# A hybrid attention block on one core: first-stage weights split earlier, dummies between two turns, latent keys and values one step sooner, latent weights by two loads

## The chip, the cores and the metric

The kernel runs on one core of one Trainium2 chip. The metric is device time in microseconds (us) of that core; lower is better. The time shown is the median of several runs on the chip, beside one further execution that was profiled and from which all rows of the trace come.

## The reference

A decoder block of depth 1 on 512 tokens of width 1024, with 16 learned tokens put in front (528 in all). In short:

```
u    = rmsnorm(h)                         # 528 x 1024
proj = u @ w_in                           # cq, ckv, k_pe, z_mla, fq, fk, fv, f, z_fox, gate_a, gate_b
q    = rmsnorm(cq) @ w_uq                 # MLA: 16 heads of 64 + 32 (rotated)
k, v = rmsnorm(ckv) @ w_ukv               # MLA: 16 heads of 64 and 64, the rotated key shared
o_mla = causal_attention(q, k, v)
o_fox = causal_attention(fq, fk, fv, with a cumulative forget gate)   # 16 heads of 64
y_mla = (o_mla * silu(z_mla)) @ w_br_mla ;  y_fox = (o_fox * silu(z_fox)) @ w_br_fox
h    += rmsnorm((sigmoid(gate_a) * y_mla + sigmoid(gate_b) * y_fox) @ w_out)
```

All in float32. `w_uq` is 256 x 1536 (16 heads of 64 + 32 columns) and `w_ukv` 128 x 2048 (16 heads of 64 key and 64 value columns). The 16 added tokens are dropped from the output.

## The kernel before

**Precision.** TensorE multiplies in a reduced float32. Each product is therefore made of three matmuls: operands are split into a high half (a cast copy) and a low half (the difference), and high x high, high x low and low x high are added in PSUM. For weights a unit loads a raw tile (`wload`, L105), casts it on ScalarE to `wh` and subtracts on GpSimd to `wl` (`wsplit`, L125). Raw, `wh` and `wl` tiles have three buffers each. `weights` (L137) makes a `get` that loads and splits once, with `get.load` for the load alone.

**Units and steps.** `unit` (L175) cuts one projection into steps of three matmuls. Its first step calls `getw()`, the split, and starts the loads of the next three units (`nxt`, set by `ahead`, L842); its last step calls `done`, which evicts the PSUM bank. The banks for these results, `acc` (L170), are three. So `z` (8 steps of 512 columns), `mq` (the MLA query, 2 steps), `mk` (MLA key, 2 short steps in two banks), `v` and so on are lists of steps, and a stage strings such lists together in a `fill`.

**Phases.** The first phase normalises the input, turns it (`turn`, L355: eight transposes by TensorE of one block of 128 tokens), and makes the small projections (`small`, L391, into `psm`; `back`, `latent`). Ten dummy matmuls into `spun` (L450) run before. Then come 16 stages, alternately forgetting attention (FoX, `br` 1) and MLA (`br` 0) for each of 8 pairs of heads. Stage 0 is FoX of pair 0, stage 1 MLA of pair 0, stage 2 FoX of pair 1, and so on. At last the branch products (`py`) and the output product (`x`, `y`, `z` tiles of that phase) follow.

**A stage** (L888 on) issues scores `s0`, the values `va` of the stage before (`late`), scores `s1`, then the steps of its `fill`, with the normalisations `n0` and `n1` (L778) put among them. The scores (`st` on TensorE) go through VectorE (`sf`, the negated maximum) and ScalarE (exponential). `norm` writes the probabilities in two half-precision halves (`pn`: high on ScalarE L801, low on VectorE L802, the first 16 keys on GpSimd L788 to L793), and starts transposing DMAs from `pn` to `pt` on the SyncE queue, two per block of 128 queries, eight per stage. `values` (L812, `ov` on TensorE) multiplies `pt` by the values `vp`, which another transposing DMA makes from `vh`. `n0` covers the first three query blocks, `n1` the fourth.

**The fill.** A FoX stage prepares its own and the next stage's gates and the MLA operands:

```
fill = (vts[br, pr] if pr else begun) + za + q + zb[:4] + k + zb[4:6] + v + zb[6:]
```

`za` is `z` of the FoX branch, `zb` of the MLA branch, `q` is `mq`, `k` is `mk` and `v` the MLA values. An MLA stage has `fq`, `fk` and `v` of the next pair. In stage 0, `fill[:5]` is issued ahead of `n0`: four steps of a gate unit (`pg`) and the first of `za`; `n0` and `n1` follow directly, and then `fill[5:]`.

**Values and z.** `v_unit` (L664) finds a power-of-two scale `vsc` on VectorE from the largest entry (L679 to L687), then writes `vh` on ScalarE (L692, L698) and VectorE (L701). `z_unit` (L710) evicts `z` as `sil` by ScalarE (L714) and VectorE (L715). `hl_done` (L234) evicts queries and keys (`hlq`, `hlk`) by ScalarE and VectorE, with a raised priority.

**What sets the order.** On TensorE the order is that of the program, written out by hand. On ScalarE, VectorE, GpSimd and partly SyncE a planner puts instructions in order by their estimated readiness and priority (`high_priority` raises it, `issue_after` makes one follow another; `pin` and `keep_in_program_order` fix the order). Each engine then runs its list strictly in that order.

**The latent weights.** `q_mla` (L579) loads, for one pair of heads, four pieces: for each of the two halves of `w_uq` 64 columns of two heads, and from `w_ukv` the key and the value columns of the two heads (512 columns in all). One cast and one subtraction split them.

Of the kernel before, what the change touches and what calls it, by code (L numbers as in the profile page):

```python
# [12 lines left out]
F32R = mybir.dt.float32r  # L13
# [18 lines left out]
NOPE = 64  # L32
ROPE = 32
HD = 64
# [15 lines left out]
def f32(ap):  # L50
    return ap.bitcast(F32)
# [3 lines left out]
def block_kernel(ctx: ExitStack, tc: tile.TileContext, x, meta_tokens, pre_norm_g, w_in, fox_forget_b,  # L55
                 mla_q_norm_g, mla_kv_norm_g, w_uq, w_ukv, w_br_mla, w_br_fox, w_out, post_norm_g,
                 rope_tok, rope_pe, out):
    nc = tc.nc
# [5 lines left out]
    wuq = w_uq[0].rearrange("(k p) f -> p k f", p=128)  # L64
    wukv = w_ukv[0]
# [17 lines left out]
    wp = ctx.enter_context(tc.tile_pool(name="wp", bufs=3))  # L83
    uid = [0]
    written, sums_out = [False], []
    behind, through, first_t, exps, halved, lowered = [], [], [], [], {}, {}
# [9 lines left out]
    def mm(*a, **k):  # L96
        nc.tensor.matmul(*a, **k)  # L97

    def tps(*a):
        nc.tensor.transpose(*a)  # L100

    def split_lo(eng, lo, src, hi):
        return eng.tensor_tensor(out=lo, in0=src, in1=f32(hi), op=ALU.subtract)  # L103

    def wload(srcs):  # L105

        uid[0] += 1
        u = uid[0]
        raw = wp.tile([128, 1024], F32, tag="wraw", name=f"wraw{u}")
        n = 0  # L110
        parts = []
        for src in srcs:
            dims = src.shape[1:]
            w = int(np.prod(dims))
            names = "abcd"[: len(dims)]
            pat = f"p ({' '.join(names)}) -> p {' '.join(names)}"
            rv = raw[:, n : n + w].rearrange(pat, **{c: d for c, d in zip(names, dims)})
            dma(rv, src)
            parts.append((n, w))
            n += w  # L120
        return u, raw, parts, n
# [15 lines left out]
    def weights(srcs, wrap):  # L137

        st = {}

        def load():
            if "l" not in st:
                st["l"] = wload(srcs())

        def get():
            load()
            return wrap(wsplit(st["l"]))
        get.load = load
        return get
# [20 lines left out]
    def acc(name):  # L170
        return accp.tile([128, 512], F32, tag="acc", name=name)
# [3 lines left out]
    def unit(name, getw, act, nk, sls, done):  # L175

        st = {}
        out = []
        for i, sl in enumerate(sls):
            n = sl.stop - sl.start  # L180
            for k in range(nk):
                def fn(i=i, sl=sl, k=k, n=n):
                    if "w" not in st:
                        st["w"] = getw()
                        for load in getattr(out[0][1], "nxt", ()):
                            load()
                    if k == 0:
                        st["ps"] = acc(f"{name}{i}")
                    ps = st["ps"][:, :n]
                    (wh, wl), (ah, al) = st["w"], act(k)  # L190
                    for q, (w, a) in enumerate(((wh, ah), (wh, al), (wl, ah))):
                        mm(ps, w(k), a[:, sl], start=(k == 0 and q == 0), stop=(k == nk - 1 and q == 2))
                    if k == nk - 1:
                        done(i, ps)
                out.append((3 * n / 2.4, fn))
        if hasattr(getw, "load"):
            out[0][1].load = getw.load
        return out
# [25 lines left out]
    CT = fx.tile([128, L], F32R, tag="CT", name="CT")  # L224
    ONE = fx.tile([128, 128], F32R, tag="ONE", name="ONE")
# [40 lines left out]
    with ExitStack() as ph:  # L266
# [64 lines left out]
        def squares(t, pin):  # L331

            rows = 128 if t < 4 else META
            ht = hts[t]
            hn = hns[t] = pa.tile([128, D], F32, tag="hn", name=f"hn{t}", bufs=3)
            st1 = sts[t] = pa.tile([128, 16], F32, tag="st1", name=f"st1_{t}")
            if t == 0:

                for i, sl in enumerate(halves):
                    pin(nc.scalar.activation(hn[:, sl], ht[:, sl], AF.Square, accum_out=st1[:, 2 + i : 3 + i]))  # L340
                pin(nc.vector.tensor_scalar(out=st1[:, 0:1], in0=st1[:, 2:3], scalar1=1.0 / D, scalar2=EPS, op0=ALU.mult,
                                            op1=ALU.add))
                pin(nc.scalar.activation(st1[:, 1:2], st1[:, 3:4], AF.Sqrt, bias=st1[:, 0:1], scale=1.0 / D))
                pin(nc.vector.reciprocal(st1[:, 1:2], st1[:, 1:2]))
            else:
                pin(nc.scalar.activation(hn[:rows], ht[:rows], AF.Square, accum_out=st1[:rows, 0:1]))
                rstd(st1[:rows, 1:2], st1[:rows, 0:1], D, 0, rows, pin)
# [7 lines left out]
        def turn(t):  # L355
            rows = 128 if t < 4 else META
            for half in range(2):

                pt = acc(f"pt{t}_{half}").rearrange("p (a b) -> p a b", a=4) if t in (1, 4) else \
                    ppt.tile([128, 4, 128], F32, tag="pt", name=f"pt{t}_{half}")  # L360
                pts0[t, half] = pt
                for kk in range(4):
                    k = 4 * half + kk
                    tps(pt[:, kk, :rows], hns[t][:rows, 128 * k : 128 * k + 128], ident[:rows, :rows])
# [84 lines left out]
        spun = acc("spun")  # L449
# [5 lines left out]
        scaled(0, pin)  # L455
        pin(nc.vector.tensor_copy(gcol, gps[:, 0, 0:KD]))
        turn(0)
        squares(1, pin)
        scaled(1, pin)
        pin(small_hi(0, nc.scalar.copy))  # L460
# [87 lines left out]
    with ExitStack() as att:  # L548
# [25 lines left out]
        wuqh = wuq.rearrange("p k (h e) -> p k h e", e=NOPE + ROPE)  # L574
# [2 lines left out]
            dma(f32(QP), qpe_dram[2 * pr : 2 * pr + 2].rearrange("h i x f s -> (h i x f) s"))  # L577

        def q_mla(pr):  # L579
            kv = wukv.rearrange("p (h a e) -> p a h e", a=2, e=HD)  # L580

            def wrap(w):
                mw[pr] = w
                return (lambda k: w[k][0]), (lambda k: w[k][1])
            get = weights(lambda: [wuqh[:, k, 2 * pr : 2 * pr + 2, 0:NOPE] for k in range(2)]
                          + [kv[:, i, 2 * pr : 2 * pr + 2, :] for i in range(2)], wrap)

            halves = hl_done(("q", 0, pr), S, S)

            def q_done(i, ps):  # L590
                halves(i, ps)
                if pr:
                    load_qp(pr)
            return unit(f"mq{pr}", get, cq_act, 2, REAL, q_done)
# [62 lines left out]
        mw = {}  # L657
# [175 lines left out]
        vts = {}  # L833
# [18 lines left out]
        begun = g[4:]  # L852
        fills = []
        for si, (br, pr) in enumerate(stages):
            last = si + 1 == len(stages)
            if not last:
                q, k, v = feed(*stages[si + 1])
            if br == 1:

                za, zb = z_unit(1, pr), z_unit(0, pr)  # L860
                fill = (vts[br, pr] if pr else begun) + za + q + zb[:4] + k + zb[4:6] + v + zb[6:]
            elif not last:

                fill = vts[br, pr] + q + k[:KD] + v + k[KD:]
            else:
                g = gate_unit()
                fill = vts[br, pr] + g + gate_unit() + gate_unit()
            if si == 5:
                pe, rest1, _ = pe_unit(1)
                fill[17:17] = pe  # L870
            fills.append(fill)
# [16 lines left out]
        for si, (br, pr) in enumerate(stages):  # L888
            s0, s1, n0, n1, va = attention(br, pr)

            fill = fills[si]
            for fn in [s0] + late:
                fn()
            if si == 0:
                run(fill[:3])
            s1()

            if si == 0:

                run(fill[3:5])  # L900
                run(vts[1, 0] + pe_rest)
                n0()
                n1()
                first_t.extend(through)
                run(fill[5:])
            else:
                if si == 1:

                    written[0] = True
                    for x in range(2):  # L910
                        store0(x, 2, 8)
                    written[0] = False
                run(fill[:5])
                if si == 1:

                    behind[:] = exps[:1]
                if si == 2:
                    behind.clear()
                n0()
                run(fill[5:11])  # L920
                if br:

                    behind[:] = [halved[("k", 1, pr), 1]]
                run(fill[11:12])
                if br:
                    behind.clear()
                n1()
                if 6 <= si < 8:

                    written[0] = True  # L930
                    rest1(si - 6)
                    written[0] = False
                run(fill[12:])
            written[0] = False
            if si == 1:

                behind[:] = [halved[("k", 1, 1), 0]]
            late = [va]
# [232 lines left out]
```

## Time and profile before

| | us |
|---|---|
| median of 3 runs | 606.51 |
| lowest and highest | 606.22 and 607.24 |
| the profiled execution's own time | 607.8 |
| its span, from first to last instruction | 606.0 |
| VectorE busy | 370.6 |
| ScalarE busy | 343.3 |
| GpSimd busy | 179.0 |

In the profile PE is TensorE's matmuls, PEld its weight loads, DVE is VectorE, ACT ScalarE, POOL GpSimd, SPq the SyncE queue that issues DMAs. A row of a timeline has the start, the duration, the engine, the line, the operation, what is written and read, the shape, the count, and in brackets the idle time of the engine before it and what ended it. A row of the waits has the waiting engine, tile and line, what it waited for, then the total, the count and the longest. A row of a group ends with busy time and mean ns of one, then idle time before them with its causes. TensorE's matmuls overlap, so a matmul's duration is longer than the step from one start to the next.

### The profile page before, as it was taken

What the parts mean: (1) busy time and instruction counts of PE and PEld (TensorE: products, weight loads), DVE (VectorE), ACT (ScalarE), POOL (GpSimd) and SP (SyncE); (2) the same over time, 40 slices, a digit from 0 to 9 for tenths busy, and PEclk for the clock granted to TensorE, in tenths of its full rate; (3) what the DMA queues carried; (4) which work ended last, traced back from release to release, by engine and by line L of the source; (5) the groups of instructions that cost most, each with busy time, mean ns of one, the idle gap of its engine ahead of it and who ended that gap; (6) DMA issues with size and microseconds to landing.
All of it is one profiled execution on the core that took longest, in us unless ns stands there. A gap on an engine that the chain in (4) does not pass through costs nothing.

```text
span 606.0 us, 11016 instructions
## 1 busy us (share of the span) xinstructions
PE 593.3 (98%) x3773; PEld 502.2 (83%) x3773; DVE 370.6 (61%) x1002; ACT 343.3 (57%) x780; POOL 179.0 (30%) x231
## 2 busy tenths in 40 slices
PE   7999999999999999999999999999999999999996
PEld 5889789789889889888798898887888888888884
DVE  4956657765775674675666557683823624367857
ACT  7847755764774685675666658671221533243653
POOL 4316626443438444353433534530000000000000
PEclk9999999999999999999999999999999999999999
DMA  8433689989798788999787786997634333332603
GB/s 292 101 89 82 132 191 166 225 175 211 118 179 162 163 191 160 193 178 191 144 151 178 148 175 158 192 167 249 210 105 104 94 82 104 104 93 92 233 0 138
DMA packets 225335, 92.71 MB, mean 153 GB/s; under 512 B 141868, under 2 KB 217012, under 8 KB 225280
## 3 DMA queue, kind: packets, MB, share of 16 engines
q1 hardware_dynamic: 225280, 92.03, 66.9%
q8 instruction: 29, 0.48, 0.3%
q14 instruction: 26, 0.21, 0.1%
HBM read 57.57 MB, written 4.00 MB: 102 GB/s over the span
## 4 chain that ended last, share of the span: by engine, by line
PE 88%; ACT 3%; DVE 3%; DMA 2%; issue 2%; POOL 0%; SPq 0%; DVEq 0%; ACTq 0%
PE z L97 15%; PE py L97 14%; PE pg L97 14%; PE v L97 9%; PE fk L97 8%; PE fq L97 7%; PE st L97 6%; PE ov L97 4%; PE x L97 4%; PE psm L97 2%; DVE sf L766 2%; PE mq L97 2%; PE mk L97 1%; DMA wsr<-in_w_in_dram 1%; PE ppe L97 1%
## 5 line engine op out<-in xcount | busy, mean ns | idle before, releaser
L130 ACT CAST wh<-wraw 128x1024 fp32r<-128x1024 f32 (+1 forms) x88 | 87.9, 1001 | 155.2 <-PE v L97 46.3
L103 POOL TENSOR_TENSOR wl<-wraw,wh 128x1024 fp32r<-128x1024 f32 (+1 forms) x55 | 121.3, 2207 | 106.6 <-ACT wh L130 106.4
L774 ACT ACTIVATE sf<-sf,nb 128x144 f32<-128x144 f32 (+3 forms) x128 | 72.0, 564 | 13.3 <-DVE nb L766 13.3
L802 DVE SCALAR_TENSOR_TENSOR pn<-sf,ri,pn 128x128 f16<-128x128 f32 (+3 forms) x128 | 68.7, 576 | 13.3 <-ACT pn L801 13.2
L801 ACT ACTIVATE pn<-sf,ri 128x128 f16<-128x128 f32 (+3 forms) x128 | 61.5, 551 | 20.4 <-ACT sf L774 17.3
L103 DVE TENSOR_TENSOR wl<-wraw,wh 128x1024 fp32r<-128x1024 f32 x33 | 40.3, 1222 | 41.3 <-ACT wh L130 41.2
L97 PE MATMUL z<-uTh,wl 128*128 128x512 f32 x128 | 50.2, 392 | 1.6 <-POOL wl L103 1.6
L97 PE MATMUL z<-uTh,wh 128*128 128x512 f32 x128 | 50.9, 398 | 0.0
L766 DVE CUSTOM_DVE_ANT_0 sf<-st,maskt 128x272 f32<-128x272 f32 (+2 forms) x128 | 48.5, 434 | 3.9 <-PE st L97 3.9
L97 PE MATMUL pg<-uTh,wh 128*128 128x512 f32 x128 | 50.3, 393 | 0.0
L97 PE MATMUL z<-uTl,wh 128*128 128x512 f32 x128 | 50.0, 391 | 0.0
L97 PE MATMUL pg<-uTl,wh 128*128 128x512 f32 x128 | 49.8, 389 | 0.0
L97 PE MATMUL pg<-uTh,wl 128*128 128x512 f32 x128 | 49.8, 389 | 0.0
L97 PE MATMUL py<-gh,wh 128*128 128x512 f32 x128 | 49.8, 389 | 0.0
L97 PE MATMUL py<-gl,wh 128*128 128x512 f32 x128 | 49.8, 389 | 0.0
L97 PE MATMUL py<-gh,wl 128*128 128x512 f32 x128 | 49.8, 389 | 0.0
L97 PE MATMUL st<-hlk,hlq 64*128 64x272 f32 (+3 forms) x480 | 49.1, 308 | 0.3
L97 PEld LDWEIGHTS st<-hlk,hlq 64*128 64x128 f32 x480 | 36.0, 185 | 7.0 <-ACT wh L130 2.5
L97 PE MATMUL v<-uTh,wh 128*128 128x256 f32 (+1 forms) x128 | 36.5, 285 | 0.0
L97 PE MATMUL v<-uTh,wl 128*128 128x256 f32 (+1 forms) x128 | 36.5, 285 | 0.0
L97 PE MATMUL fk<-uTl,wh 128*128 128x256 f32 (+1 forms) x128 | 36.4, 285 | 0.0
L97 PE MATMUL fk<-uTh,wh 128*128 128x256 f32 (+1 forms) x128 | 36.4, 285 | 0.0
(232 smaller groups left out, 1403.4 us busy)
## 6 DMA issues: line engine op xcount, KB each, us to landing
wraw<-in_w_in_dram SPq DMA_DIRECT2D x56, 512.0 KB
wraw<-in_w_br_fox_dram SPq DMA_DIRECT2D x8, 512.0 KB
tb<-in_w_out_dram SPq DMA_DIRECT2D x8, 512.0 KB
wraw<-in_w_br_mla_dram SPq DMA_DIRECT2D x8, 512.0 KB
wraw<-in_w_out_dram SPq DMA_DIRECT2D x6, 512.0 KB
pt<-pn SPq DMA_TRANSPOSE x128
xr<-in_x_dram SPq DMA_DIRECT2D x4, 512.0 KB
out_dram<-yo SPq DMA_DIRECT2D x8, 256.0 KB
```

What stands on the lines that cost most here:

```text
L97: nc.tensor.matmul(*a, **k)
L103: return eng.tensor_tensor(out=lo, in0=src, in1=f32(hi), op=ALU.subtract)
L130: nc.scalar.copy(wh[:, :n], raw[:, :n])
L766: nc.vector.tensor_tensor_reduce(out=sf_of(h, b)[:, c0 : c0 + w], in0=ps[h][:, o : o + w], in1=maskt[:, m0 : m0 + w], scale=-scale, scalar ...
L774: exps[g] = nc.scalar.activation(sf, sf, AF.Exp, bias=sums["nb"][:, h, b : b + 1], scale=-1.0, accum_out=sums["su"][:, h, b : b + 1]).ins
L801: nc.scalar.activation(hi, sf, AF.Copy, scale=rib)
L802: nc.vector.scalar_tensor_tensor(out=lo, in0=sf, scalar=rib, in1=hi, op0=ALU.mult, op1=ALU.subtract)
```

## The change

Four edits. (1) Each unit's first step gets a function `prep` that makes the split ahead of the step; in stage 0 the first two units of `fill[5:]` (`mq0` and the first `zb`, called `z00`) are prepared between `n0` and `n1`. (2) Four more dummies into `spun` follow `turn(0)`. (3) In a FoX stage `k` and `v` come one `zb` step sooner. (4) `q_mla` loads two pieces, 192 columns from each half of `w_uq` (with the 32 rotated ones per head, which aren't used here) in one DMA and 256 adjacent columns of `w_ukv` in another, 640 columns in all. Two casts and two subtractions pick the 512 wanted ones out.

```diff
@@ unit
+        def prep():
+            if "w" not in st:
+                st["w"] = getw()
+            return True
...
-                    if "w" not in st:
-                        st["w"] = getw()
+                    if "b" not in st:
+                        st["b"] = prep()
                         for load in getattr(out[0][1], "nxt", ()):
                             load()
...
+        out[0][1].prep = prep
@@ first phase
         turn(0)
+        for _ in range(4):
+            mm(spun, ONE, CT[:, 0:512], start=True, stop=True)
         squares(1, pin)
@@ q_mla
-            kv = wukv.rearrange("p (h a e) -> p a h e", a=2, e=HD)
-
-            def wrap(w):
-                mw[pr] = w
+            ld = []
+
+            def load():
+                if not ld:
+                    ld.append(wload([wuq[:, :, 192 * pr : 192 * pr + 192], wukv[:, 256 * pr : 256 * pr + 256]]))
+
+            def get():
+                load()
+                u, raw, _, _ = ld[0]
+                wh, wl = (wp.tile([128, 1024], F32R, tag=t, name=f"{t}{u}") for t in ("wh", "wl"))
+                cuts = [(raw[:, 0:384].rearrange("p (b e) -> p b e", e=96)[:, :, 0:NOPE], lambda t: t[:, 0:256].rearrange("p (b e) -> p b e", e=NOPE)),
+                        (raw[:, 384:640].rearrange("p (h a e) -> p a h e", h=2, a=2), lambda t: t[:, 256:512].rearrange("p (a h e) -> p a h e", a=2, h=2))]
+                for src, to in cuts:
+                    with tc.issue_after(behind[0]) if behind else nullcontext():
+                        nc.scalar.copy(to(wh), src)
+                for src, to in cuts:
+                    split_lo(nc.gpsimd, to(wl), src, to(wh))
+                w = mw[pr] = [(wh[:, o : o + 128], wl[:, o : o + 128]) for o in range(0, 512, 128)]
                 return (lambda k: w[k][0]), (lambda k: w[k][1])
-            get = weights(lambda: [wuqh[:, k, 2 * pr : 2 * pr + 2, 0:NOPE] for k in range(2)]
-                          + [kv[:, i, 2 * pr : 2 * pr + 2, :] for i in range(2)], wrap)
+            get.load = load
@@ fill of a FoX stage
-                fill = (vts[br, pr] if pr else begun) + za + q + zb[:4] + k + zb[4:6] + v + zb[6:]
+                fill = (vts[br, pr] if pr else begun) + za + q + zb[:3] + k + zb[3:5] + v + zb[5:]
@@ stage 0
                 n0()
+                for ahead_ in [fn.prep for _, fn in fill[5:] if hasattr(fn, "prep")][:2]:
+                    ahead_()
                 n1()
```

## The prediction

> **What bounds the kernel now.** I read the page's busy times first, then the waits of TensorE, then the timelines around each of those waits, engine by engine.
>
> ```profile
> PE 593.3 (98%) x3773; PEld 502.2 (83%) x3773; DVE 370.6 (61%) x1002; ACT 343.3 (57%) x780; POOL 179.0 (30%) x231
> ```
>
> ```profile
> PE z L97 <- POOL wl L103: 1.6, 1, 1.6
> PE ov L97 <- DMA pt<-pn: 0.9, 2, 0.5
> PE ov L97 <- issue: 0.7, 2, 0.4
> ```
>
> TensorE is busy for 98% of the span, so the change can only win what TensorE idles, and it adds no matmul but four dummies. The largest waits are one for a low half of weights (1.6 us, in stage 0) and two sets in front of `ov`, the product of probabilities and values. Matmuls that start late without an idle row cost a little more; I find those by comparing equal stretches, below.
>
> **Part 1: weights ahead of the last normalisation.** The 1.6 us wait, with what ScalarE and GpSimd did before it:
>
> ```profile
> 64.78 1.30 POOL L103 TENSOR_TENSOR wl<-wraw,wh 128x512 fp32r<-128x512 f32 x1
> ...
> 71.33 1.34 ACT L801 ACTIVATE pn<-sf,ri 128x512 f16<-128x512 f32 x2 [0.47 <-DVE ri L783]
> 72.57 1.03 ACT L130 CAST wh<-wraw 128x1024 fp32r<-128x1024 f32 x1
> ...
> 73.68 2.37 POOL L103 TENSOR_TENSOR wl<-wraw,wh 128x1024 fp32r<-128x1024 f32 x1 [1.44 <-ACT wh L130]
> ...
> 74.14 0.39 PE L97 MATMUL z<-uTl,wh 128*128 128x512 f32 x1
> 76.11 0.50 PE L97 MATMUL z<-uTh,wl 128*128 128x512 f32 x1 [1.57 <-POOL wl L103]
> ```
>
> ```profile
> 112.39 5.65 PE z L97 x24
> ```
>
> The row from the chain has 24 matmuls of 512 columns in 5.65 us: one starts 0.235 us after another, so the one at 76.11 was due at 74.14 + 0.23 = 74.37: 1.74 us are lost. Of the two units prepared early, `mq0` is halved early in the old order already (512 columns, on GpSimd until 66.08); `z00` is the one that counts. Its cast now precedes the two `pn` of `n1` (1.34 us). ScalarE is free 0.47 us before 71.33, at 70.86, so the cast ends about 71.9 and the subtraction, 2.37 us later, about 74.3, when TensorE wants it: −1.74 us in stage 0. The four small GpSimd pieces of `n1` come either before or after it; if before, some 0.3 us of the wait stay. What is pushed back is `n1`: its `pn` come about 1.1 us later, and their two transposing DMAs are the last of eight in a row on the SyncE queue, which holds 11.10 us from 69.22 and reaches the seventh at 69.22 + 6 x 1.39 = 77.6. `pn` is done by 75, so nothing is late there.
>
> The Trainium skill ("SBUF — State Buffer", section "Who interferes with whom") says that a VectorE instruction with two SBUF inputs and a GpSimd instruction that reads SBUF exclude one another. By it the moved subtraction would hold `pn` on VectorE (1.42 us) until 74.3, and `hlq` behind it until 77.1, so that `mk` would wait 0.7 us for its bank and part 1 would be worth −1.0 instead of −1.74; the sum would stay, since stage 1 keeps less than that of either (part 2), but a sum in which stage 1 keeps all would be 0.7 us poorer. The trace agrees with the rule in this row against this mean, while a GpSimd subtraction ran from 90.48:
>
> ```profile
> 91.31 1.91 DVE L802 SCALAR_TENSOR_TENSOR pn<-sf,ri,pn 128x256 f16<-128x256 f32 x1
> ...
> L802 DVE SCALAR_TENSOR_TENSOR pn<-sf,ri,pn 128x256 f16<-128x256 f32 x32 | 17.3, 561 | 0.0
> ```
>
> **Part 2: how much of it survives stage 1, and the two loads.** The next wait of TensorE is at the values of stage 1, and it hangs on the SyncE queue:
>
> ```profile
> 69.22 11.10 SPq L91 DMA_TRANSPOSE pt<-pn  x8
> 80.37 1.27 SPq L91 DMA_DIRECT2D wraw<-in_w_in_dram  x2
> 81.69 4.50 SPq L91 DMA_DIRECT2D qpe_dram<-gT  x4
> ...
> 87.12 3.07 SPq L91 DMA_TRANSPOSE vp<-vh  x1
> ...
> 91.69 2.87 SPq L91 DMA_TRANSPOSE pt<-pn  x2
> 94.65 1.05 SPq L91 DMA_DIRECT2D wraw<-in_w_uq_dram  x2
> 95.80 1.21 SPq L91 DMA_TRANSPOSE pt<-pn  x1
> 97.06 1.08 SPq L91 DMA_DIRECT2D wraw<-in_w_ukv_dram  x2
> 98.25 4.57 SPq L91 DMA_TRANSPOSE pt<-pn  x3
> 102.90 0.53 SPq L91 DMA_DIRECT2D wraw<-in_w_in_dram  x1
> 103.60 3.45 SPq L91 DMA_TRANSPOSE pt<-pn  x2
> ```
>
> ```profile
> 108.39 0.38 PE L97 MATMUL ov<-pt,vp 80*64 80x512 f16 x1 [0.48 <-DMA pt<-pn]
> 109.19 2.03 PE L97 MATMUL ov<-pt,vp 80*64 80x512 f16 x25 [0.42 <-DMA pt<-pn]
> ```
>
> The reader is to see that the queue has hardly a gap from 69 to 107: each row starts where the one before ended (the two rows left out fill 86.3 to 87.0 and 90.3 to 91.5). The last two transposes go out from 103.60 on, and TensorE waits for the landing of the one at 108.39 and of the other at 109.19. So up to 109.19 the queue, not TensorE, sets the time, and what stage 0 wins would only lengthen these two waits. But the four loads of `mq1` stand in this queue, ahead of those transposes: from 94.65 to 95.80 and from 97.06 to 98.25, 2.34 us. With two loads instead of four I take half away, 1.17 us. From above: those loads bring 128 x 8 runs of 64 numbers, the new ones 128 x 3 of 192 or 256, and a transpose just behind the loads is slower (three of them in 4.57 us, against 3 x 1.21), so up to 0.94 us more may go, 2.1 us. From below: if the queue's pace is set by the transfers and not by the issues, nothing. I take 1.17, as the nearest rows have it. The second wait then ends at 108.0, and TensorE, there 1.74 us earlier, does wait: parts 1 and 2 together give −1.17 us, and the other 0.57 us of part 1 are given back.
>
> In later pairs a shorter queue wins only where TensorE waits for it; the waits above name four in front of `ov`, two of them these, so I take nothing there. The cast of `mq` becomes two casts of 256 columns and two subtractions. What a second instruction adds, from rows of 512 and 1024: on ScalarE 2 x 0.63 − 1.03 = 0.23 us, on GpSimd 2 x 1.30 − 2.37 = 0.23 us. The old casts stand where ScalarE had been idle:
>
> ```profile
> L130 ACT CAST wh<-wraw 128x512 fp32r<-128x512 f32 x10 | 6.3, 627 | 38.5 <-PE v L97 34.6 <-issue 3.6 <-PE z L97 0.2
> ```
>
> That idle time, 38.5 us before ten casts, hides them; without it the two would cost 0.46 us a pair, 3.7 us in all.
>
> **Part 3: latent keys and values one z step sooner.** A z step is three matmuls, 0.7 us. The order of TensorE's work changes but not its amount. At the start of an MLA stage the rows are these:
>
> ```profile
> 126.18 0.16 DVE L687 RECIPROCAL vsc<-vsc 128x1 f32<-128x1 f32 x1
> 126.29 1.05 ACT L130 CAST wh<-wraw 128x1024 fp32r<-128x1024 f32 x1 [0.22 <-PE z L97]
> 127.24 0.59 ACT L714 ACTIVATE sil<-z 128x512 f32<-128x512 f32 x1
> 127.73 0.28 ACT L692 ACTIVATE vh<-v,vsc 128x32 f16<-128x32 f32 x1
> ...
> 130.63 0.72 PE L97 MATMUL st<-hlk,hlq 64*128 64x272 f32 x6
> 132.48 0.50 PE L97 MATMUL fq<-uTh,wh 128*128 128x512 f32 x1
> ...
> 173.22 0.65 PE L97 MATMUL st<-hlk,hlq 64*128 64x272 f32 x6
> ...
> 174.63 0.50 PE L97 MATMUL fq<-uTh,wh 128*128 128x512 f32 x1
> ```
>
> The second cast waits for the end of `z` and holds `sil` and the eviction of the values (`vh`) behind it; VectorE's `sf` comes after both, and the scores wait for a PSUM bank: 130.63 to 132.48 is 1.85 us. In the stage at 173.22, where the second cast has only 512 columns, the same stretch is 1.41. So 0.44 us go in each stage of the slow kind; four stretches of that length are in the timeline, from 130.63, 218.11, 346.26 and 388.77: 1.76 us. The scale of the values (`vsc`) is ready at 126.34 now, just after `z` ends at 126.3. With `v` 0.7 us sooner it is ready about 125.65, and the order of ScalarE, which is planned by when work comes ready, should put `vh` into the idle time there and leave only the cast and `sil` behind `z`. VectorE then does `vh` a microsecond sooner and reaches `sf` about 1.5 us sooner, more than the 0.44 us: −1.76 us. If the order on ScalarE stays, `vh` still waits behind the cast and nothing is won. What is queued behind: the second cast slips by up to 0.7 us, for `fk`, whose matmuls come 6 us later.
>
> The price is in PSUM. `mk` takes over the banks of `mq` and of the z before. In stage 4:
>
> ```profile
> 163.47 0.68 DVE L103 TENSOR_TENSOR hlq<-mq,hlq 128x512 fp32r<-128x512 f32 x1
> ...
> 164.94 0.28 PE L97 MATMUL mk<-cTh,wh 128*128 128x256 f32 x1
> ```
>
> `mq` is evicted at 164.15; `mk`'s second half, moved to 164.94 − 0.69 = 164.25 (three matmuls of 0.23), comes 0.10 us after that. It fits, barely. I take the five FoX stages after it as like it, cost it at nothing, and at most 0.1 us x 6 for the release itself.
>
> **Part 4: four dummies.** `turn(1)` waits for `hn`, and TensorE is idle for 0.59 us before it:
>
> ```profile
> 2.07 4.63 PE L97 MATMUL spun<-CT,ONE 128*128 128x512 f32 x10 [2.07 <-DVE ONE L230]
> ...
> 8.77 1.09 PE L100 MATMUL pt<-ident,hn 128*128 128x128 f32 x8 [0.59 <-DVE hn L352]
> ...
> 12.81 2.17 ACT L376 ACTIVATE uTh<-pt,gcol 128x128 fp32r<-128x128 f32 x8
> ```
>
> At 0.23 us each they end at 9.1, at the 0.46 of the first ten at 10.0: `turn(1)` ends up to 1.3 us later, at most 11.2, and ScalarE reads it at 12.81. Nothing is lost, and as the cast of the last weights, not TensorE, sets when ScalarE comes to it, nothing is won: 0, from −0.2 to +0.3.
>
> **Sum.** −1.17 − 1.76 = −2.9 us. The profiled execution took 607.8 us, of which the span is 606.0; it lies 1.3 us above the median, 606.51, and the terms are taken off that median: 603.6 us, a span of 603.1.
>
> **Rivals.**
> *The transfers, not the issues, pace the queue.* Then two loads win nothing there, and all of part 1 is given back at 109: 606.5 − 1.76 = 604.7 us. For it: transposes behind loads are slower than others. Against: between the loads they go at 1.21 each, as fast as any. The Trainium skill ("DMA: Bandwidth & Descriptors", section "Anatomy of one DMA — SWDGE (gpsimd) path") has the fixed cost of a DMA mostly in its completion and little in its issue; by that this rival's time would hold, but the rows above show half a microsecond of the queue for each.
> *ScalarE's order stays.* `vh` remains behind the cast; only −1.17: 605.3 us. For it: in the old order it stands there although its scale was ready at 126.34, and the new 125.65 may not count for the planner.
> *Both:* 606.5, no change, and the change doesn't do what it says.
> *Slower: the bank of `mq` isn't free.* The margin is 0.10 us. If the new order puts one cast of 1.05 us ahead of `hlq` on ScalarE, `mk` waits 0.95 us in each of six stages: +5.7 − 2.9, 609.3 us. It decides from a delay of more than 0.10 us, and loses from 0.6 us on. For it: ScalarE is in order and its order is made anew; against: the eviction has a raised priority.
>
> **How the numbers follow.** Forecast 603.6: 0.42; transfers 604.7: 0.15; ScalarE's order 605.3: 0.18; both fail 606.5: 0.10; slower 609.3 or on the way there: 0.15. 0.2% is 1.2 us, about what can be told from no change; the boundary, 605.3, halves the third case. Faster 0.42 + 0.15 + 0.09 = 0.66, same 0.09 + 0.10 = 0.19, slower 0.15. The range: below, 2.1 for the queue plus 1.76 plus what shorter waits before `ov` elsewhere may give (0.7 us), 602.0; above, no gain and the bank's 0.6 us, 607.1. It leaves out most of the slower case.
>
> **What would show it.** Right: no row of `z` waiting for `wl` near 74; two loads of `in_w_uq` and `in_w_ukv` for each pair and the second wait of `ov` ending near 108.0; `vh` ahead of `sil` on ScalarE, and 1.41 us from `st` to `fq` in all MLA stages. Wrong: a new wait of `mk` for `hlq` or `sil`; the `ov` of stage 1 still at 109; longer waits of `ov` in later FoX stages, where the old ones (0.7 us in two) show how tight the landing is.

## The result, and the profile after

| | us |
|---|---|
| after, median of 13 runs | 604.04 (602.86 to 607.24) |
| before, median of 13 runs, the three of 606.51 among them | 607.62 (606.22 to 609.08) |
| ratio after to before, 95% interval | 0.9949 (0.9936 to 0.9963) |
| the profiled execution after, its span | 603.71, 601.8 |

The change makes the kernel faster by 0.5%: 0.0051 x 607.62 = 3.1 us, from 2.2 to 3.9 by the interval. Forecast were 2.9 us and 603.6. In the profiles of after and of the experiments some lines have other numbers: `pn` is L822 and L823, `sil` L735 and L736, `vh` L713, L719 and L722, the VectorE `sf` L787.

Busy times and the waits of TensorE, after. A row of the waits has the total, the count and the longest:

```profile
PE 592.5 (98%) x3777; PEld 501.7 (83%) x3777; DVE 374.1 (62%) x1002; ACT 343.9 (57%) x788; POOL 180.6 (30%) x239
```

```profile
PE ov L97 <- DMA pt<-pn: 0.3, 1, 0.3
PE z L97 <- POOL wl L103: 0.3, 1, 0.3
```

The 1.6 us wait for `wl` has become 0.3, and the 1.6 us in front of `ov` have become 0.3. Part 1, in the timeline of stage 0 after:

```profile
70.67 1.04 ACT L130 CAST wh<-wraw 128x1024 fp32r<-128x1024 f32 x1
...
71.29 0.24 POOL L809 TENSOR_TENSOR mt<-sf,ri 128x32 f32<-128x32 f32 x1 [3.62 <-DVE ri L804]
...
72.11 2.40 POOL L103 TENSOR_TENSOR wl<-wraw,wh 128x1024 fp32r<-128x1024 f32 x1
...
72.36 3.37 DVE L823 SCALAR_TENSOR_TENSOR pn<-sf,ri,pn 128x512 f16<-128x512 f32 x2 [1.22 <-ACT pn L822]
...
73.90 0.39 PE L97 MATMUL z<-uTl,wh 128*128 128x512 f32 x1
74.57 0.50 PE L97 MATMUL z<-uTh,wl 128*128 128x512 f32 x1 [0.28 <-POOL wl L103]
...
76.25 0.68 DVE L103 TENSOR_TENSOR hlq<-mq,hlq 128x512 fp32r<-128x512 f32 x1
76.38 0.39 PE L97 MATMUL mk<-cTh,wh 128*128 128x272 f32 x1
...
76.98 0.38 PE L97 MATMUL mk<-cTh,wh 128*128 128x256 f32 x1
```

The cast is ahead of the two `pn` of ScalarE. The subtraction starts at 72.11, behind `n1`'s small GpSimd pieces, and `z` has its low half at 74.57, 0.44 us after it was due (73.90 + 0.23). Beside the subtraction VectorE's two `pn` take 3.37 us (1.42 before), so `hlq` ends at 76.93 and the second half of `mk` starts only then. Stage 0, from its first scores to those of stage 1, takes 21.02 us after and 21.93 before (81.69 − 60.67 and 82.84 − 60.91): 0.91 are won, of 1.74 forecast. Of the rest 0.44 stayed at `z`, and 0.39 went at `mk`: from 76.31, when it was due (76.08 + 0.23), to the `z` behind it at 77.44 it takes 1.13 us, before 0.74 (78.50 to 79.24).

Part 2, the SyncE queue of stage 1 after, and TensorE behind it:

```profile
85.57 3.89 SPq L91 DMA_TRANSPOSE vp<-vh  x1
...
90.61 2.81 SPq L91 DMA_TRANSPOSE pt<-pn  x2
93.51 0.53 SPq L91 DMA_DIRECT2D wraw<-in_w_uq_dram  x1
94.09 0.46 SPq L91 DMA_DIRECT2D wraw<-in_w_ukv_dram  x1
94.66 1.20 SPq L91 DMA_TRANSPOSE pt<-pn  x1
95.95 0.53 SPq L91 DMA_DIRECT2D QP<-qpe_dram  x1
96.57 4.54 SPq L91 DMA_TRANSPOSE pt<-pn  x3
101.20 0.53 SPq L91 DMA_DIRECT2D wraw<-in_w_in_dram  x1
101.84 3.41 SPq L91 DMA_TRANSPOSE pt<-pn  x2
```

```profile
106.60 0.40 PE L97 MATMUL ov<-pt,vp 80*64 80x512 f16 x1
107.30 2.01 PE L97 MATMUL ov<-pt,vp 80*64 80x512 f16 x25 [0.30 <-DMA pt<-pn]
```

The four loads' 2.34 us have become 1.15 (93.51 to 94.66), as forecast. But the load of `QP`, behind the last transposes before, now stands ahead of five of them and takes 0.62 back. From the start of `vp` to the end of the last transposes the queue takes 19.68 us after (85.57 to 105.25) and 19.93 before (87.12 to 107.05): 0.25 us, not 1.17. But `vp` itself, ahead of the loads, is 0.82 us longer; from its end it is 15.79 us after and 16.86 before, 1.07 less. The second wait of `ov` ends at 107.30, for 109.19 before and 108.0 forecast.

Part 3, ScalarE and TensorE at the start of an MLA stage after:

```profile
123.61 0.17 DVE L708 RECIPROCAL vsc<-vsc 128x1 f32<-128x1 f32 x1
...
123.81 0.29 ACT L713 ACTIVATE vh<-v,vsc 128x32 f16<-128x32 f32 x1 [0.31 <-DVE vsc L708]
...
124.70 0.60 ACT L735 ACTIVATE sil<-z 128x512 f32<-128x512 f32 x1
...
125.18 1.06 ACT L130 CAST wh<-wraw 128x1024 fp32r<-128x1024 f32 x1
...
128.74 0.65 PE L97 MATMUL st<-hlk,hlq 64*128 64x272 f32 x6
...
130.17 0.50 PE L97 MATMUL fq<-uTh,wh 128*128 128x512 f32 x1
```

`vh` comes as soon as `vsc` is ready, ahead of `sil` and of the second cast, which was first before. From `st` to `fq` it is 1.43 us instead of 1.85, here and in the stretches from 216.04, 342.86 and 385.00. Part 4: the dummies lie between the two turns, and `turn(1)` starts at 8.72 instead of 8.77.

```profile
7.34 1.18 PE L97 MATMUL spun<-CT,ONE 128*128 128x512 f32 x4
8.72 1.09 PE L100 MATMUL pt<-ident,hn 128*128 128x128 f32 x8 [0.20 <-DVE hn L358]
```

### The profile page after: what moved, and what is told of

Read it like the earlier page. It is cut to its first block, busy times and chain, and to the rows that moved or that the text cites. A ratio compares the mean times of both kernels' runs of the same rounds, so it can differ in the third digit from the quotient of the medians.

```text
span 601.8 us, 10999 instructions
## 1 busy us (share of the span) xinstructions
PE 592.5 (98%) x3777; PEld 501.7 (83%) x3777; DVE 374.1 (62%) x1002; ACT 343.9 (57%) x788; POOL 180.6 (30%) x239
## 4 chain that ended last, share of the span: by engine, by line
PE 92%; ACT 3%; DMA 2%; DVE 1%; issue 1%; POOL 1%; SPq 0%; DVEq 0%; ACTq 0%; POOLq 0%
PE z L97 16%; PE py L97 14%; PE pg L97 14%; PE v L97 9%; PE st L97 8%; PE fq L97 8%; PE fk L97 7%; PE ov L97 5%; PE x L97 4%; PE psm L97 2%; PE mq L97 2%; PE mk L97 1%; PE ppe L97 1%; DMA wsr<-in_w_in_dram 1%; PE y L97 1%; DMA ht<-in_x_dram 1%
## 5 line engine op out<-in xcount | busy, mean ns | idle before, releaser
L103 POOL TENSOR_TENSOR wl<-wraw,wh 128x1024 fp32r<-128x1024 f32 (+2 forms) x63 | 122.6, 1954 | 105.3 <-ACT wh L130 76.5
L130 ACT CAST wh<-wraw 128x1024 fp32r<-128x1024 f32 (+1 forms) x80 | 83.1, 1042 | 115.7 <-PE pg L97 38.6
L823 DVE SCALAR_TENSOR_TENSOR pn<-sf,ri,pn 128x128 f16<-128x128 f32 (+3 forms) x128 | 70.7, 592 | 13.9 <-ACT pn L822 13.8
L822 ACT ACTIVATE pn<-sf,ri 128x128 f16<-128x128 f32 (+3 forms) x128 | 61.5, 551 | 20.4 <-ACT sf L795 17.6
L787 DVE CUSTOM_DVE_ANT_0 sf<-st,maskt 128x272 f32<-128x272 f32 (+2 forms) x128 | 48.6, 435 | 3.9 <-PE st L97 3.9
L97 PE MATMUL st<-hlk,hlq 64*128 64x272 f32 (+3 forms) x480 | 47.3, 306 | 0.0
L700 DVE TENSOR_REDUCE vsc<-v 128x1 f32<-128x272 f32 (+1 forms) x32 | 13.2, 432 | 37.9 <-PE v L97 37.9
```

The lines of the kernel that those rows point to most:

```text
L130: nc.scalar.copy(wh[:, :n], raw[:, :n])
L700: nc.vector.tensor_reduce(out=sc[:, i : i + 1], in_=ps, op=ALU.max, axis=AX.X, apply_absolute_value=True)
L787: nc.vector.tensor_tensor_reduce(out=sf_of(h, b)[:, c0 : c0 + w], in0=ps[h][:, o : o + w], in1=maskt[:, m0 : m0 + w], scale=-scale, scalar ...
L822: nc.scalar.activation(hi, sf, AF.Copy, scale=rib)
L823: nc.vector.scalar_tensor_tensor(out=lo, in0=sf, scalar=rib, in1=hi, op0=ALU.mult, op1=ALU.subtract)
```

## The experiments

The theory was that of the prediction: the order on ScalarE shortens the MLA stages, the SyncE queue decides how much of stage 0's gain is left, and `mk` has next to no margin. The rivals are named with each run. Differences in us are the ratio applied to the median of the kernel before in the same batch, which was 606.8 to 607.9.

### The four parts alone

Edits: `e1_step` has only the changed `fill` line of a FoX stage, `e2_loads` only the new `q_mla`, `e3_ahead` only `prep` and its loop, `e4_dummies` only the dummies.

```diff
+ fill = (vts[br, pr] if pr else begun) + za + q + zb[:3] + k + zb[3:5] + v + zb[5:]           # e1_step
+ ld.append(wload([wuq[:, :, 192 * pr : 192 * pr + 192], wukv[:, 256 * pr : 256 * pr + 256]]))  # e2_loads
+ for ahead_ in [fn.prep for _, fn in fill[5:] if hasattr(fn, "prep")][:2]: ahead_()           # e3_ahead
+ for _ in range(4): mm(spun, ONE, CT[:, 0:512], start=True, stop=True)                        # e4_dummies
```

> The kernel before with latent keys and values one z step sooner, nothing else. My theory: the scale of the values is ready before z ends, ScalarE writes vh ahead of the cast and of sil, and the stretch from the second scores to fq falls from 1.85 to 1.43 us in the four slow MLA stages: -1.7 us by itself, and up to 1 us more if the waits of the product with the values in two later FoX stages go too. Stage 0 and the wait at the values of stage 1 stay as they were. Rival (the banks of mq are too late): the four stretches shorten but mk waits in six stages and the time stays within 0.6 us. Rival (the order on ScalarE does not depend on the step): 0.

> The kernel before with the two-load latent weights, nothing else. My theory: the SyncE queue is what sets the end of the two waits at the values of stage 1, and it gets 1.2 to 1.8 us shorter ahead of them; TensorE loses 1.35 us there, so the second wait ends some 1.2 to 1.35 us sooner and the time falls by 1.2 to 1.35 us. Stage 0 keeps its wait for the low half, and the four slow stretches stay at 1.85. Rival (the transfers and not the issues pace the queue): the wait stays, 0.

> The kernel before with the first two weight units of stage 0 split ahead of the last normalisation, nothing else. My theory: the wait for the low half falls from 1.6 to about 0.3 us, mk then waits for its banks because VectorE's norm is held by the GpSimd subtraction, so stage 0 ends 0.9 us sooner; the SyncE queue is no shorter, so the waits at the values of stage 1 grow by as much and nothing of it is left at 112: 0 us in all. Rival (the queue follows TensorE): the 0.9 us stay, -0.9.

> The kernel before with the four dummies between two turns, nothing else. My theory: 0 us, the first scores of stage 0 start at 60.9 as before, since the cast of the last small weights sets the pace there. Rival (the dummies keep the clock up or let it rise sooner): the first scores start 0.25 us or more sooner, as in the changed kernel, and that stays to the end: -0.25 us.

| | median, us | ratio to before, 95% | difference |
|---|---|---|---|
| e1_step | 605.57 (604.48 to 607.31) | 0.9969 (0.9955 to 0.9983) | −1.9 |
| e2_loads | 607.89 (606.99 to 608.78) | 1.0003 (0.9990 to 1.0015) | +0.2 |
| e3_ahead | 607.35 (606.05 to 609.83) | 1.0001 (0.9987 to 1.0015) | +0.1 |
| e4_dummies | 607.34 (605.88 to 609.65) | 0.9994 (0.9977 to 1.0011) | −0.4, the interval holds 1 |

Only part 3 does anything by itself, and with the forecast size (−1.76). Part 1 alone shortens stage 0 to 20.46 us (81.18 − 60.72), by 1.47, more than in the whole: `z` is only 0.26 us late, and without the moved step `mk` is issued 0.7 us later and waits for nothing. Yet nothing of it is in the median. In its trace the waits before `ov` of stage 1 are there as before, but 1.6 us sooner:

```profile
106.85 0.38 PE L97 MATMUL ov<-pt,vp 80*64 80x512 f16 x1 [0.60 <-DMA pt<-pn]
107.61 2.04 PE L97 MATMUL ov<-pt,vp 80*64 80x512 f16 x25 [0.38 <-DMA pt<-pn]
```

Where the 1.47 us go is not shown. From the first scores of stage 0 to those of stage 3 it is 64.07 us in this trace and 65.46 before: this execution (606.32 us, 1.0 below its median) kept nearly all of it. But in the trace of `e4_dummies`, which leaves the program of these stages as it was, no row has `ov` waiting, stage 2 is 19.46 us (20.41 before), and the same stretch is 64.53; the time, 605.88 us, is the lowest of its runs. So the waits on which part 2 of the prediction rests differ from one execution to the next, and one trace of each kernel can't say what a change does to them. The rival of `e4` is not borne out either: the first scores come 0.44 us sooner in its trace, but over all traces they come between 60.47 and 62.31 with the dummies, and between 60.56 and 61.01 without.

### Two parts, and the whole without one

`e5_ahead_loads` is parts 1 and 2 together. `e6_no_loads` is the whole without part 2, `e9_no_ahead` the whole without part 1.

```diff
-                for ahead_ in [fn.prep for _, fn in fill[5:] if hasattr(fn, "prep")][:2]:   # e9_no_ahead, from the whole
-                    ahead_()
```

> Parts 1 and 2 together (weights ahead, two loads), without the other two. My theory, that the SyncE queue takes back at stage 1's values what stage 0 wins unless the queue is shorter: each alone measured nothing (ratios 1.0001 and 1.0003), together about -1.0 us, a ratio near 0.998, with the second ov of stage 1 starting its work about 1.2 us or more sooner than before (109.19). Rival, the two add up as they did alone: 1.000 within its interval, and stage 1's values still wait some 2 us longer than the stage needs.

> The whole change without the two loads (parts 1, 3 and 4). My theory: part 1 is given back at stage 1's values and only part 3 is left, -1.9 us, a ratio near 0.997. Rival, the two loads are worth nothing in the whole either: it stays at the whole change's -3.1 us, 0.995.

> The whole change without the weights ahead (parts 2, 3 and 4). The whole was -3.1 us, parts 1, 3 and 4 together -1.2 to -1.5. My theory, that the two loads count only where the rest of a stage has become shorter than its SyncE queue (part 3 does that in every MLA stage): parts 2 and 3 together keep most of it, about -2.4 us, ratio 0.996, and part 1 is worth the remaining 0.7. Rival, it takes all three: without part 1 only part 3's -1.7 is left, ratio 0.997, as for part 3 alone. Stage 0 shows its 1.6 us wait for wl again under both.

| | median, us | ratio to before, 95% | difference |
|---|---|---|---|
| e5_ahead_loads (1, 2) | 607.83 (606.64 to 611.22) | 1.0010 (0.9994 to 1.0025) | +0.6 |
| e6_no_loads (1, 3, 4) | 606.99 (604.82 to 608.87) | 0.9981 (0.9962 to 0.9999) | −1.2 |
| e9_no_ahead (2, 3, 4) | 605.30 (603.82 to 606.83) | 0.9953 (0.9933 to 0.9973) | −2.9 |
| the whole (1, 2, 3, 4) | 604.04 (602.86 to 607.24) | 0.9949 (0.9936 to 0.9963) | −3.1 |

`e5` misses my expectation of −1.0: its interval ends at −0.4 us. So parts 1 and 2 bring nothing as a pair that the median shows. Its trace does have the second `ov` of stage 1 at 107.35 instead of 109.19, but then a wait of 1.00 us in stage 9, where before waited 0.35; the execution, 606.82 us, is 1.0 below its median:

```profile
107.35 0.62 PE L97 MATMUL ov<-pt,vp 80*64 80x512 f16 x4 [0.60 <-DMA pt<-pn]
...
258.50 0.84 PE L97 MATMUL ov<-pt,vp 80*64 80x512 f16 x6 [1.00 <-issue]
```

`e6` falls short of the whole, and the two intervals only touch: where part 3 is there, the two loads are worth 1.9 us, some ±1.4 by the two intervals. `e9` comes out near my number: part 1 is worth 0.2 us in the whole, with an interval of some ±1.5. The trace of `e6` shows a cost that the whole doesn't have. The SyncE queue ends the transposes of stage 1 at 106.93 instead of 105.25; 1.24 us of this it is late already at `vp` (86.81 for 85.57), ahead of the four loads, so they are not all of it. TensorE comes to the values of stage 1 as early as in the whole and waits twice:

```profile
108.25 0.38 PE L97 MATMUL ov<-pt,vp 80*64 80x512 f16 x1 [1.53 <-DMA pt<-pn]
109.03 3.42 PE L97 MATMUL ov<-pt,vp 80*64 80x512 f16 x25 [0.40 <-DMA pt<-pn]
112.38 0.87 PE L97 MATMUL st<-hlk,hlq 64*128 64x272 f32 x6
```

The reader is to see the 3.42 us, for 2.01 after: TensorE was slow there. A table by stretches (time, busy TensorE, VectorE, ScalarE and GpSimd with their counts, the granted clock, DMA share, GB/s) has the clock:

```profile
106.80:108.20 1.40, 0.00 (x0) 0.00 (x0) 1.40 (x8) 1.27 (x3) 0.15 (x1) 1.00 1.28 275
108.20:109.00 0.80, 0.38 (x1) 0.11 (x1) 0.18 (x2) 0.80 (x5) 0.80 (x1) 1.00 1.05 192
109.00:111.00 2.00, 1.97 (x14) 1.29 (x16) 0.00 (x0) 2.00 (x8) 1.41 (x1) 0.62 1.11 348
111.00:112.30 1.30, 1.30 (x15) 1.10 (x11) 0.36 (x2) 0.79 (x4) 0.65 (x3) 0.50 1.01 262
```

After 1.93 us of waiting the granted clock was 0.50, so the wait cost a second time. That is one execution; that this event makes the difference between `e6` and the whole in the median is argued, not shown.

### How large the margin of mk is

`e7_two_steps` moves keys and values one more step ahead.

```diff
-                fill = (vts[br, pr] if pr else begun) + za + q + zb[:3] + k + zb[3:5] + v + zb[5:]
+                fill = (vts[br, pr] if pr else begun) + za + q + zb[:2] + k + zb[2:4] + v + zb[4:]
```

> The whole change, but latent keys and values two z steps sooner instead of one. If the margin at the bank of mq is as small as the traces show (after: mk right behind the end of hlq, less than 0.1 us lost), one more step of 0.7 us makes mk wait some 0.6 us for hlq in each of six to eight FoX stages: 4 us slower than the whole change, a ratio to before of about 1.001, with new rows of mk waiting for hlq. Rival, the planner or the pairs' spare time takes it in: no new wait, ratio 0.995 as the whole change.

608.07 us (607.64 to 609.06), ratio 1.0001 (0.9984 to 1.0019): 4.0 us above the whole change's median and 3.2 by the two ratios, near the 4 expected. The waits have the new row, and `mk` idles in all eight FoX stages:

```profile
PE mk L97 <- DVE sil L736: 2.4, 8, 0.6
```

FoX stages, from first scores to first scores, take 19.78 us in this trace, 19.14 in the whole and 19.09 before. So one step costs 0.05 us a stage and the next 0.64: the margin of 0.10 us was read rightly. Something else is told here: no `ov` waits in this trace, and the runs lie within 1.4 us, where those of the whole lie within 4.4. With 0.6 us more in every FoX stage the transposes were there in time in this trace, and the small scatter of the runs fits that.

### The order on ScalarE without the step

`e8_vh_first` is the kernel before, with the cast for `fk` held until after `vh`; `e11_after_vh` is the whole change with this in place of the moved step.

```diff
-                    nc.scalar.activation(hi, p, AF.Copy, scale=sc[:, 3:4])
+                    vhs[br, pr] = nc.scalar.activation(hi, p, AF.Copy, scale=sc[:, 3:4]).ins
...
-                run(fill[5:11])
+                run(fill[5:9])
+                held = behind[:]
+                if not br and not last and not held:
+                    behind[:] = [vhs[br, pr]]
+                run(fill[9:11])
+                behind[:] = held
```

> The kernel before with no step moved: only the cast of fk's weights is made to follow the last vh on ScalarE (the planner then puts both casts behind sil and vh). If part 3's gain comes from the order on ScalarE alone, the stretch from st to fq shrinks from 1.85 to about 1.43 us in the four slow MLA stages without moving keys and values: -1.7 us, ratio 0.997. Rival, the values have to come a step sooner for it, since vsc is ready only when z ends: stretches stay at 1.85, ratio 1.000. A price may show: the casts are some 2 us later, and a wait of fq for its low half would cost up to 0.5 us a stage.

> The whole change with part 3 put another way: keys and values stay at their old steps, and the cast of fk's weights follows the last vh instead. Theory: the order on ScalarE is what shortens the MLA stages (it did so in the run before, 23.03 us for 23.44), and the earlier step costs 0.05 us in each FoX stage plus 0.5 us in stage 0, where mk waits for the bank of mq; so this is 0.5 to 0.9 us better than the whole change, ratio 0.994. Rival, sooner values also start the transposes of vh and pn sooner, which the SyncE queue needs: the waits before ov come back and it is no better than 0.996.

`e8`: 606.93 us, ratio 0.9981 (0.9966 to 0.9995), −1.2 us; the −1.7 expected lies in the interval (−2.1 to −0.3). Its MLA stage with both steps as before:

```profile
126.25 0.84 ACT L698 ACTIVATE vh<-v,vsc 128x256 f16<-128x256 f32 x2
126.96 2.01 ACT L130 CAST wh<-wraw 128x1024 fp32r<-128x1024 f32 x2
```

```profile
129.84 0.65 PE L97 MATMUL st<-hlk,hlq 64*128 64x272 f32 x6
...
131.26 0.50 PE L97 MATMUL fq<-uTh,wh 128*128 128x512 f32 x1
```

The stretch is 1.42 us although no step has moved, so the order on ScalarE is what shortens it; the rival of sooner values falls. `e11` should then have been better than the whole by 0.5 to 0.9. It isn't: 606.14 us, 0.9968 (0.9950 to 0.9986). In its trace `mk` waits for nothing and stage 0 takes 20.61 us, but there are 3.1 us of waits before `ov`. The rival, that sooner values also start the transposes sooner, allowed no better than 0.996 and fits. Whether the waits come with the later `vh` or were chance in that execution is open.

### Whether the issues or the transfers pace the queue

`e10_gp_queue` issues the loads of `QP` and of the two rows of `CT` on GpSimd; `e12_gp_some` leaves the `QP` loads of pairs 1 and 4 on SyncE.

```diff
-                        dma(f32(CT[64 * h : 64 * h + 2, :]), c_dram[:, 2 * pr + h, :])
+                        dma(f32(CT[64 * h : 64 * h + 2, :]), c_dram[:, 2 * pr + h, :], nc.gpsimd.dma_start)
...
-            dma(f32(QP), qpe_dram[2 * pr : 2 * pr + 2].rearrange("h i x f s -> (h i x f) s"))
+            dma(f32(QP), qpe_dram[2 * pr : 2 * pr + 2].rearrange("h i x f s -> (h i x f) s"), None if pr in (1, 4) else nc.gpsimd.dma_start)
```

> The whole change, with the loads of QP and of CT's rows issued on GpSimd's queue instead of SyncE's (nothing else on SyncE changes). Theory, that the pace of the SyncE queue sets the waits before ov in stages 2, 8 and 10 and the scatter from run to run: the queue has some 1.3 us less to issue in a FoX stage (0.53 or 0.35 for QP, two of 0.40 for CT) and 0.6 less ahead of stage 1's last transposes, so these waits shrink, the runs lie closer together, and the median falls by 0.5 to 1.5 us, ratio 0.992 to 0.994. Rival, the landing of the transposes (the transfers) sets the waits, not the issue: no change, 0.995. A price: each issue holds GpSimd for a time that no run here has shown; if it is over 1 us and falls ahead of its pieces of pn, the transposes start later and it is slower, 0.997 or above.

> As the run with GpSimd's queue, but the QP loads of pairs 1 and 4 are back on SyncE: their data are written only just before (GpSimd stood 11.6 us on the one of pair 4 in stage 8, and mk behind it 3.05 us; 2.0 us on the one of pair 1). All other loads of QP and CT stay on GpSimd, where they lay in its idle time (0.64 us for QP, 1.09 for two of CT). Theory, that the issues of the SyncE queue make the waits before ov of stages 8 and 10: 5 us of stage 8 are gone, those two waits stay away (3.6 and 2.7 us at worst elsewhere, 1.97 without a wait), the scatter of the runs is smaller, and the median is 0.5 to 1.5 us under the whole change's: ratio 0.9925 to 0.994. Rival, the transfers pace it, as the stage 1 of that run suggests (22.1 us of queue from the first vp to the last pt, for 19.7 in the whole change, with fewer issues): no better than 0.995.

`e10`: 607.84 us (604.69 to 611.60), ratio 0.9996 (0.9972 to 1.0020). The price was not the issue itself but what stood behind it. In the trace, which is of the run of 611.60 us, GpSimd stood 11.59 us on a load of `qpe_dram`, whose last writes SyncE issued only at 234.24 to 235.49. Its three subtractions then ran one behind the other from 242.13 to 246.13, and VectorE's `su`, 0.17 us in this stage of the whole, took 3.65 beside them. The `pn`, the cast and the `sil` of ScalarE came later with it, and TensorE idled 3.05 us at `mk`:

```profile
241.47 0.64 POOL L91 DMA_DIRECT2D QP<-qpe_dram  x1 [11.59 <-PE ov L97]
242.13 1.44 POOL L103 TENSOR_TENSOR wl<-wraw,wh 128x256 fp32r<-128x256 f32 x2
...
243.73 2.40 POOL L103 TENSOR_TENSOR wl<-wraw,wh 128x1024 fp32r<-128x1024 f32 x1
```

```profile
242.53 3.65 DVE L803 TENSOR_SCALAR su<-su 128x6 f32<-128x6 f32 x1 [1.27 <-ACT sf L795]
```

```profile
254.91 0.39 PE L97 MATMUL mk<-cTh,wh 128*128 128x272 f32 x1 [3.05 <-DVE sil L736]
```

`e12` takes that away: 604.39 us (603.65 to 604.88 in 6 runs), ratio 0.9956 (0.9942 to 0.9970). No `ov` waits for the values of stages 8 and 10 (nor does one in the trace of the whole), and the runs lie within 1.2 us, which fits that part of the theory. The time is not better than the whole's. In stage 0 GpSimd, which has issued the two loads of `CT` there, starts its small pieces 0.52 us after `ri` (0.15 in the whole), the subtraction comes behind the start of VectorE's `pn` and takes 2.87 us for 2.40, and the wait for the low half of `z` is 1.1 us again. In stage 1 the queue has two issues fewer ahead of the last transposes, the rows of `CT`, of which one lay in the stretch from `vp` on, and the stretch is longer, 20.66 us (85.29 to 105.95) for 19.68:

```profile
85.29 4.25 SPq L91 DMA_TRANSPOSE vp<-vh  x1
...
90.36 3.46 SPq L91 DMA_TRANSPOSE pt<-pn  x2
...
102.31 3.64 SPq L91 DMA_TRANSPOSE pt<-pn  x2
```

Here the first issues that are left grow by more than was taken away: `vp` from 3.89 to 4.25, the two `pt` behind it from 2.81 to 3.46. The same stretch was 19.5 to 20.1 us in the six traces with four loads (before, `e1`, `e3`, `e4`, `e6`, `e8`) and 18.9 to 20.3 in the six with two (`e2`, `e5`, `e7`, `e9`, `e11`, the whole). From the end of `vp` it was 16.1 to 16.9 and 15.6 to 16.3, with 17.65 in `e11`. So the two loads do take something off the queue, and part of it comes back in the first transposes. That the transfers pace those fits this, but is not shown. The Trainium skill ("DMA: Bandwidth & Descriptors", section "Issuing engines are not separate DMA queues") says that DMAs of all issuing engines run on the same sixteen engines; this stretch, no shorter with loads moved to GpSimd, is in line with it.

## Why the prediction was right, and where it wasn't

**The bound** was read rightly: what was won is TensorE's waits, its busy time is 592.5 us for 593.3.

**Part 1** was right in its mechanism and too large in its size. Of 1.74 us, 0.44 stayed in the whole, and 0.26 with part 1 alone, because GpSimd's small pieces came first, which the prediction named at 0.3. Another 0.39 us went in the whole, where `mk` comes a step sooner and waits for the banks of `z` and `mq`. The prediction had this wait by the rule of the Trainium skill ("SBUF — State Buffer", section "Who interferes with whom"): `hlq` held until 77.1, `mk` 0.7 us late. Measured: 76.93, and 0.39. The trace agrees with the rule, 3.37 us of `pn` beside the subtraction for 1.42 without. That part 1 alone is worth nothing was right in the median (+0.1 us). That it is lost at the values of stage 1 is not shown: in the trace of part 1 alone stage 2, which computes them, is 20.49 us, before 20.41.

**Part 2** is the step that failed: "With two loads instead of four I take half away, 1.17 us", and from it "parts 1 and 2 together give −1.17 us". The pair measured +0.6 us (−0.4 to +1.5). The queue itself did much of what was forecast: the issues shrank by 1.19 us, `QP`'s load moved in (0.62), and behind `vp` the stretch is 1.07 us shorter. What the prediction had wrong is the wait that this was to shorten. It read two waits of `ov` in one trace, 0.90 us together, as a fixed cost of stage 1. In the trace of `e4` no row has them though no load was taken away, in that of `e6` they are 1.93 us, and in that of `e5` a wait of 1.00 us stands in stage 9, where the prediction took nothing. Which of these waits make up the median is open. The rival "the transfers, not the issues, pace the queue" had nothing for the two loads, as they measured alone (+0.2 us), but only −1.76 for the whole, outside the interval.

That the sum came out all the same is in part luck: the four parts alone add up to −2.0 us, the whole is −3.1. The loads seem to count where part 3 is there: 1.9 us between `e6` and the whole, about 1.0 between `e1` and `e9` (whose intervals overlap, and which differ by the dummies too). What in part 3 makes them count isn't settled. The extra casts show in no wait, as forecast.

**Part 3** was right: −1.76 forecast, −1.9 measured (−2.7 to −1.0) alone, 0.42 us in each of four stretches, by the order on ScalarE, and the margin of `mk` was as small as read. Against it each FoX stage is 0.05 us longer, less than the 0.1 allowed. The step is one way to this order and not the only one, as `e8` shows. And four stages are not all: in the trace of `e4`, where `ov` doesn't wait, the stretches of stages 9 and 11 are long too, 1.84 and 1.77 us, while before, behind the waits of `ov`, they are 1.42 and 1.41.

**Part 4** was right: nothing that stands out of the scatter.

**The sum**, −2.9 us, stands against −3.1 (−3.9 to −2.2). The rival that ended slower, a late bank of `mq`, didn't come; `e7` shows that it was one step away.

## What to carry to other kernels

An equal stretch of TensorE that is longer in some stages than in others points to an order on another engine; here a cast ahead of a small eviction cost 0.42 us a stage, and the order alone gave it back. A saving of issues on a DMA queue is one only if the issues that are left don't grow: compare the whole stretch, not the rows removed. A wait that one trace shows need not be in the next execution: look for it in several traces before a term rests on it. Parts measured alone don't add up where a wait sits between them, so the whole must also be measured without each part.

## What the runs showed of the hardware

A short idle of TensorE cost twice in two executions here. After the 3.05 us at `mk` in `e10` it ran on for 0.85 us, and then its clock was halved for 3.4 us, from 255.76 to 259.17 in stretches of 0.2 us; here in longer ones:

```profile
254.90:256.10 1.20, 1.19 (x6) 1.01 (x7) 0.65 (x2) 0.39 (x1) 1.19 (x1) 0.86 0.84 160
256.10:258.70 2.60, 2.60 (x9) 2.02 (x8) 0.77 (x2) 0.37 (x1) 0.00 (x0) 0.50 0.97 185
259.60:261.70 2.10, 2.10 (x11) 1.55 (x10) 1.36 (x6) 1.62 (x4) 0.80 (x1) 1.00 1.01 240
```

The `z` matmuls at 256.13 and 256.56 are 0.43 us apart, for 0.23 else. Half of 3.4 us, about 1.7 us as an estimate, comes on top of the wait. In `e6` waits of 1.53 and 0.40 us with one matmul between were enough. The Trainium skill ("TensorE: Matmul & The Clock Gate", section "What's actually happening") has the clock halved after an idle window of about 3.4 us; the length of the halved stretch agrees, but here 1.93 us of idling sufficed. In other traces waits of 0.66 and 0.96 us (`e8`, stage 9) and of 1.19 and 0.60 (`e11`, stage 2), each with a little work between, left the clock at 1.00.

A DMA issue on GpSimd took 0.64 us for `QP` and about 0.56 for a `CT` row, against 0.53 or 0.35 and 0.40 on SyncE. What made it dear in `e10` was the wait of 11.59 us in front of one load, which held GpSimd's subtractions behind it, and VectorE's 3.65 us beside them.
